# Attention scores of a hybrid layer: the low half of the keys in a whole 128-row tile

## The chip, the cores and the metric

The kernel runs on one core of one Trainium2 chip. The metric is the device time of one execution in microseconds (us). The engines are TensorE (PE; its weight loads stand apart as PEld), VectorE (DVE), ScalarE (ACT), GpSimd (POOL) and SyncE (SP), which issues the DMAs. Each works off its own queue in order and waits on the others by semaphores.

## The reference, cut to what matters

A sequence of 512 tokens with 1024 features goes through six sublayers with modulated norms (feed-forward, pooling, latent attention) and then through two hybrid layers. A hybrid layer has two attentions on one projection: stick-breaking attention (8 heads of 64) and native sparse attention (NSA: 8 query heads of 64 in 2 groups, each group with one head of keys and values). NSA has a compressed, a selected and a window branch. With 512 tokens there are 8 blocks of 64, and the 8 best are selected, which is all of them; the window has 512 tokens. So both branches are causal attention over all keys, each with its own keys:

```python
q = rope(rms_norm(split_heads(n_q, NSA_HEADS), q_norm_g), pos)
k_slc = rope(rms_norm(split_heads(n_ks, NSA_KV_HEADS), k_norm_g[1]), pos)
k_win = rope(rms_norm(split_heads(n_kw, NSA_KV_HEADS), k_norm_g[2]), pos)
...
ss = jnp.einsum('bgrqd,bgqkd->bgrqk', qb, ks) * scale
ps = masked_softmax(ss, (tok <= tq[:, None])[:, :, None])
o_s = jnp.einsum('bgrqk,bgqkd->bgrqd', ps.astype(vs.dtype), vs)
...
sw = jnp.einsum('bgrqd,bgkd->bgrqk', qb, kw) * scale
pw = masked_softmax(sw, mw)
o_w = jnp.einsum('bgrqk,bgkd->bgrqd', pw.astype(vw.dtype), vw)
```

## The kernel before, in words

Everything is float32 in value. A product is made of operands split in two, a high part h (rounded to the format in which TensorE multiplies) and a low part l, the rest. The program writes out the order of all work by hand: the instructions of each engine stand in its queue in the order in which the Python code issues them. A layer is a list of items (`Item`), and `drive` calls them one after the other and splits and loads weights a little ahead. The DMAs of weights stand on SP's queue.

**Selected and window branches.** There are 32 units a layer: 4 query heads j of a group, times 2 groups g, times 2 branches b (selected, window), times 2 halves gr of the queries. A unit has two query tiles of 128: gr 0 those that see 128 and 256 keys, gr 1 those that see 384 and 512. `attend` pipelines the units by steps in the order of the string NSO, "HES1LNPMO0T": S scores on TensorE (`NS`, for the unit one ahead), M row maximum on DVE (`NM`), E exponential on ACT (`NE`), N scaling on DVE and POOL (`NN`), T transposes on TensorE, H and L their evacuation and split on ACT and DVE, P product with the values on TensorE (three units behind), O fold of the result. The steps "1" and "0" are gaps in which other work stands, mostly quarters of projections for a gate (tile `gx`, L256 to L258). The scores of a gr 0 unit go to a single bank, tile `s`; those of gr 1 to the only pair of banks, tile `ps`.

**Where the scores' operands lie.** Queries and keys have 64 features, half of TensorE's 128 rows. The tile of a group's queries (qA, qB) holds on the 64 rows of the group (`rows(g)`) the high part and on the other 64 rows the low part. The tile of high keys, `kth` (`st["kh"]`), holds the same high part on both halves. So one product over 128 rows gives h·h + l·h. The third part, high queries with low keys, is a second product over the group's 64 rows alone; its keys are in `ktl` (`st["kl"]`), where the two groups lie in the two halves of the rows. `scores` (L1201) takes these terms: for each of the two query tiles it issues one product per term (L1208) and then adds the causal mask by a product with the identity (L1210 for gr 1, L1213 for gr 0), which has 128 rows. The queries are the operand that is loaded into the array (LDWEIGHTS), the keys the one that streams. In the stick-breaking attention the same function gets three terms that all have 64 rows (`S_`, L1380).

**Preparation.** `prep` (L1482) opens the pools of the branch when stick-breaking's are closed: `nsa` (P) for what lives on, `nsap` (PP) for what only the preparation needs, which closes at the first score unit; its room is then taken by `nsa2` with pA and pB, the split weights of the compressed branch. `prep` also loads `y`, the bias of the compression (L1500, later its hidden layer), and has `kr`, the compressed keys. Then it starts the norms and rotations of the keys and the first queries (`norm_rope`), whose powers are made on POOL (`rpow`, L277 and L278) and whose results DVE takes (L1134). `keys` (L1600) turns the keys, and writes `kth` on ACT and `ktl` on DVE (L1611).

Of the kernel before, what the change touches and what calls it, by code (L numbers as in the profile page):

```python
# [9 lines left out]
F32 = mybir.dt.float32  # L10
# [27 lines left out]
def band_constants():  # L38
    """Row tile j of the pooling matrices of the groups side by side, columns from BAND0[j]."""
    out = np.zeros((4, 128, BANDO[4]), np.float32)  # L40
    s = np.arange(S)
    for g, w in enumerate(WINDOWS):
        lo, hi = np.clip(s - w // 2, 0, S), np.clip(s + w // 2, 0, S)
        m = ((s[:, None] >= lo[None, :]) & (s[:, None] < hi[None, :])) / (hi - lo)[None, :]
        m = (m - np.eye(S)).astype(np.float32)
        for j in range(4):
            out[g, :, BANDO[j]:BANDO[j + 1]] = m[128 * j:128 * j + 128, BAND0[j]:BAND0[j] + BANDN[j]]
    return out


def constants():
    """Arrays that depend on the shapes alone."""
# [31 lines left out]
class Chunk:  # L84
    """One load of weights into a slot or two; parts: (destination view of the slots, source)."""
# [5 lines left out]
class Half:  # L91
    """A split operand of at most 1024 columns, from a part of a chunk; chunk None: only the room."""
# [13 lines left out]
class Kern:  # L106
# [22 lines left out]
    def cols(self, w, c0):  # L129
        """256 columns of w [1024, n]: halves of 128 columns, [128, 8, 128]."""  # L130
# [5 lines left out]
    def solo(shape, *parts, late=99, eng=None):  # L136
        """A half with a load of its own; parts: (columns of the slot, shape, source)."""
# [4 lines left out]
    def cols_k(self, w, c0):  # L142
        """256 columns of w [1024, n]: halves of four row tiles, [128, 4, 256]."""
        src = lambda m: w[512 * m:512 * m + 512, c0:c0 + 256].rearrange("(k p) n -> p k n", p=128)
        return [self.solo((4, 256), (slice(0, D), (4, 256), src(m))) for m in range(2)]

    def cols_q(self, w, c0):
        """128 columns of w [1024, n] from c0 and from c0 + 256: halves of four row tiles, [128, 4, 256]."""
# [8 lines left out]
    def rows_of(self, w, j):  # L157
        """Row tiles 2j and 2j + 1 of w [n, 1024]: halves of [128, 1024]."""
        return [self.solo((D,), (slice(0, D), (D,), w[j * 256 + m * 128:j * 256 + m * 128 + 128])) for m in range(2)]

    def place(self):
        """Where the next load goes: the next slot, or pair of slots, of a ring."""
# [73 lines left out]
    def warm(self, out, n):  # L236
        """Products of no use that keep the tensor engine's clock up through a wait; out [128, 512] is written anew afterwards."""
# [9 lines left out]
    def splits(self, *parts):  # L247
        """Splits whose sources may share a tile."""
# [11 lines left out]
    def mm2(self, out, v, xh, xl, start, stop):  # L260
        """out[0:64] + out[64:128] is the product; v [K, 128] holds h and l of 64 columns."""
# [4 lines left out]
    def fold(self, po, r, y=None):  # L266
        """po[0:64] + po[64:128] on the rows r of y or of a new tile."""
# [6 lines left out]
    def rpow(self, s, mul, add):  # L274
        """s <- (s * mul + add) ** -0.5, in place"""
# [12 lines left out]
    def take(self, tag):  # L288
        """Before a room is taken again, the chain that reads it is brought to its end."""
# [8 lines left out]
    def banks(self, kind=None):  # L298
        """PSUM: four pairs of banks; mla: two pairs and four single banks; hyb: a pair and six."""
# [7 lines left out]
    def scrt(self):  # L307
        """One of three rooms, of four in the second block."""
# [10 lines left out]
    def sigmoid_steps(self, dst, x, also=None):  # L319
        """dst <- exp(min(x, 0) - ln(1 + exp(-|x|)))."""  # L320
# [13 lines left out]
    def ada(self, i, j, which, g, m, form="row", pool=None, tiles=1, tag="adaw", ahead=0):  # L334
        """Steps towards modulation vector j of layer i: as rows, or as columns [128, 8] for rows later;
        itself (g None) or 1 + itself times the gains g."""
# [39 lines left out]
    def to_row(self, acc, which, g, m, gb=None):  # L376
        """The sum over partitions of acc [128, 1024] on every partition."""
# [25 lines left out]
    def spread(self, which, g, m):  # L403
        """Rows from columns."""
# [21 lines left out]
    def border(self, m, nxt):  # L426
        """The steps of a token tile into the next sublayer: scale of the norm, modulation, turn, split."""
# [42 lines left out]
    def finale(self, product, P1, Z, X, nxt, m2, kinds):  # L470
        """The last products of a sublayer token tile by token tile, with the border behind them.
        product(t, part) in two parts; P1, Z and X bring y into the residual."""
# [36 lines left out]
    def updater(self, m, kind):  # L509
        """x += weight * c * normed(y), or x += y / 4."""  # L510
# [21 lines left out]
    def out_items(self, w, part, last, before=None, after=None, late=99):  # L532
        """part(k) -> split [128, 512] of feature tile k; last(product)."""
# [129 lines left out]
    def pool(self, cur, last):  # L663
# [17 lines left out]
        def band(g, z, js, first, last_):  # L681
            """Tokens 256 z and on of the group's pooled input from the token tiles js."""
# [33 lines left out]
        def low(h, l, src, eng):  # L716
            """Only the first and the last token's eight divide by other than powers of two."""
# [18 lines left out]
        def scale(m):  # L736
            """The map and its bias times the channels' scale."""
# [34 lines left out]
    @staticmethod  # L772
    def parts(*parts):
        """A step's other work from (lane, function, weights, steps for which they stay)."""
# [6 lines left out]
    def attend(self, n, steps, order, slices):  # L781
        """Items of a pipeline over n units: steps[letter] = (function, offset), in the order given; digits:
        slices[step] = (lists of other work for the gaps, weights)."""
# [254 lines left out]
    def trig(self, ang, cos, sin, n, r):  # L1038
        """cos and sin of ang (float32), by a reduction with an exact split of 2 pi."""
# [23 lines left out]
    def trig_tables(self, C):  # L1063
        """Steps towards the cosines and sines of the second block."""
# [29 lines left out]
    def rope_rows(self, C, l):  # L1094
        """Rotary tables with the norms' gains inside: q, k of selection, k of window, compressed k."""
# [23 lines left out]
    def norm_rope(self, src, dst, tabs, c):  # L1119
        """Rows of src [128, t, h, 64] normed over 64 (c 1: and times 1 / 8), turned, into dst (same shape)."""  # L1120
# [22 lines left out]
    def chain(self, g, *tiles):  # L1143
        """Opens a chain of operations that reads the banks."""
# [7 lines left out]
    def follow(self, g):  # L1152
        """The next step of a chain."""
# [9 lines left out]
    def advance(self, n=1):  # L1163
        """The next step of every open chain of operations."""
# [9 lines left out]
    def chunk2(self, w, c0, c1, n=128):  # L1174
        """n columns of w [1024, m] from c0 and n from c1: two halves [128, 8, n]."""
# [3 lines left out]
    def token_proj(self, h, ws, ts, ps, o=0, heads=False):  # L1179
        """Token tiles ts x 256 columns into ps[:, t + o]; ws: halves of four row tiles; heads: columns (g, j, d) as (j, g, d)."""  # L1180
# [7 lines left out]
    def feat_proj(self, out, h, w, ks=range(8)):  # L1188
        """128 columns, features on partitions, [128, 512 tokens]."""
# [7 lines left out]
    def spans(self, g):  # L1197
        """The two query tiles of group g in a packed [128, 1024]."""
        return [slice(self.off(g, i), self.off(g, i) + 128 * (2 * g + i + 1)) for i in range(2)]

    def scores(self, terms, g, mask):  # L1201
        """Masked scores of the query tiles 2g and 2g + 1, packed side by side: sums of q^T k over terms (q, k)."""
# [13 lines left out]
    def turn_steps(self, un, U, P):  # L1216
        """Steps over units un[u] = {p: packed}: transposes, evacuation, product with the values."""
# [26 lines left out]
    def causal_pv(self, po, d, v, g, first, last):  # L1244
        """po [128, 256 queries of group g] += v^T p^T; v(k) [128 keys, h | l]."""
# [6 lines left out]
    def hybrid(self, cur, l, last):  # L1252
        """Items of a layer of the second block."""
# [5 lines left out]
        # -- stick-breaking attention  # L1259
# [30 lines left out]
        def FP(pr, z, ks, bank=None):  # L1290
            """Queries (z = 0) or keys of a pair of heads, row tiles ks; pr 4: inputs of the compression."""
# [24 lines left out]
        def GA(b, ks, bank=None):  # L1316
            """Columns of the first gate ahead of their turn."""
# [8 lines left out]
        def GZ(b, ks):  # L1326
            """Stick-breaking's gate for the heads 2b and 2b + 1, on their output."""
# [10 lines left out]
        def silu_chain(b, z):  # L1338
            """oa[:, b] *= 2 z sigmoid(z)"""
# [97 lines left out]
        def two(z, tags):  # L1437
            """A product with 256 columns, token tiles in two banks."""
# [13 lines left out]
        # -- native sparse attention: preparation  # L1452
# [13 lines left out]
        def q_chain(jp, ps, ts):  # L1466
            """Queries 2 jp and 2 jp + 1 of both groups, from ps [128, t, 256] (j, g, d)."""
# [14 lines left out]
        def prep(*ws):  # L1482
# [6 lines left out]
            st["kh"], st["kl"] = P.tile([128, 2, 2, 512], F32R, name="kth"), P.tile([128, 2, 512], F32R, name="ktl")  # L1489
# [6 lines left out]
            st["kr"] = P.tile([64, 64], F32, name="kr")  # L1496
            y = P.tile([128, 256], F32, name="y")
# [40 lines left out]
        def window(z):  # L1538
            """Keys and values of the window, gates of the branches, two token tiles."""
# [60 lines left out]
        def keys():  # L1600
# [8 lines left out]
            for b in range(2):  # L1609
                for g in range(2):  # L1610
                    nc.vector.tensor_tensor(st["kl"][rows(g), b], pt[b][rows(g)], st["kh"][rows(g), b, g].bitcast(F32), op=OP.subtract)  # L1611
# [94 lines left out]
        # -- native sparse attention: selected and window branches  # L1706
# [4 lines left out]
        def NS(u):  # L1711
# [5 lines left out]
            q, r = st["qB" if j > 1 else "qA"][g][:, j % 2], rows(g)  # L1717
            nu[u] = {"s": self.scores([(q, st["kh"][:, b, g]), (q[r], st["kl"][r, b])], gr, self.causal)}
# [56 lines left out]
        # -- gates, up-projections, output  # L1775
# [89 lines left out]
    def group(names, jobs):  # L1865
        """The jobs of the names one after the other, with their weights."""
# [8 lines left out]
    def open_x(self):  # L1875
        """Room of the residual."""
        self.x = self.xs.enter_context(self.tc.tile_pool(name="x", bufs=1, side="right")).tile([128, NT, D], F32, name="x")

    def park_x(self):
        """The residual leaves the core's memory while a layer of the second block needs the room."""  # L1880
# [212 lines left out]
```

## Time and profile before

| what | value |
|---|---|
| runs, us | 3033.26, 3033.55, 3036.77 (median 3033.55) |
| profiled execution, span | 3036.1 us; no other time of it is given |
| PE busy | 2888.1 us (95%) |
| PEld busy | 2403.2 us (79%) |
| DVE busy | 1612.7 us (53%) |
| ACT busy | 1164.8 us (38%) |
| POOL busy | 396.9 us (13%) |
| chain that ended last | PE 85%, DVE 8%, ACT 3%, POOL 2% |
| mean granted clock of TensorE | 0.960 |

The busy time of an engine is the sum over its instructions, the share is that of the span. Matmuls are pipelined and the profile models their ends, so a matmul's row overlaps the next one's; what a product costs in a row of products is the distance from its start to the next start. The granted clock is 1.00 at 2.4 GHz and 0.50 at 1.2 GHz. The chain that ended last is followed back from the last instruction, at each step to what released it. The runs lie within 0.12% of each other.

### The profile page before, as it was taken

How to read it: one execution, taken by the hardware profiler on the slowest of the kernel's cores; microseconds unless marked ns; L12 is line 12 of the kernel's file. 1: busy time of each engine (PE TensorE's matmuls, PEld its weight loads, DVE VectorE, ACT ScalarE, POOL GpSimd, SP SyncE). 2: the span in 40 equal slices, each digit the busy share in tenths (PEclk: the TensorE clock that was granted, in tenths of full speed). 3: DMA queues.
4: the chain of work that ended last, by engine and by line, in shares of the span. 5: the costliest groups of instructions: out<-in, count | busy, mean ns of one | idle time of the engine just before them, and what ended most of it. 6: DMA issues, size and time to landing. Idle time of an engine off the chain costs nothing.

```text
span 3036.1 us, 35669 instructions
## 1 busy us (share of the span) xinstructions
PE 2888.1 (95%) x14135; PEld 2403.2 (79%) x14135; DVE 1612.7 (53%) x2147; ACT 1164.8 (38%) x1946; POOL 396.9 (13%) x446
## 2 busy tenths in 40 slices
PE   7999988999999999899899999998999999889999
PEld 6888877888888888778788888787777887867787
DVE  6554355443364543579642234675665438756543
ACT  4223233222231222378422233563544338444431
POOL 1000031000010000267200000111230010112200
PEclk9999989999999999899999999998799999978999
DMA  7665313543246643110243332233102431320022
GB/s 260 217 196 166 110 59 113 179 156 115 88 130 206 215 160 94 33 41 15 84 153 98 103 111 71 75 94 85 29 15 84 146 93 57 88 64 28 28 94 100
DMA packets 232661, 322.60 MB, mean 106 GB/s; under 512 B 10823, under 2 KB 194331, under 8 KB 232494
## 3 DMA queue, kind: packets, MB, share of 16 engines
q1 hardware_dynamic: 230910, 314.55, 32.3%
q10 hardware_dynamic: 1584, 5.77, 0.5%
q8 instruction: 112, 1.84, 0.3%
q14 instruction: 55, 0.45, 0.0%
HBM read 313.99 MB, written 6.29 MB: 105 GB/s over the span
## 4 chain that ended last, share of the span: by engine, by line
PE 85%; DVE 8%; ACT 3%; POOL 2%; issue 2%; DMA 0%; POOLq 0%; SPq 0%; DVEq 0%; ACTq 0%
PE ps L256 21%; PE ps L257 21%; PE ps L258 21%; PE ps L1208 2%; PE gx L256 2%; PE gx L258 2%; PE gx L257 2%; PE pt L1227 2%; PE po L264 1%; PE s L1208 1%; PE po L263 1%; PE ps L1210 1%; DVE mx L970 1%; DVE wl L1006 1%; PE pt L1652 1%
## 5 line engine op out<-in xcount | busy, mean ns | idle before, releaser
L245 DVE TENSOR_TENSOR wl<-wraw,wh 128x1024 fp32r<-128x1024 f32 (+3 forms) x414 | 496.2, 1214 | 560.1 <-ACT wh L244 559.9
L256 PE MATMUL ps<-hh,wh 128*128 128x512 f32 (+1 forms) x1696 | 659.7, 389 | 8.2 <-DVE ob L271 2.8
L257 PE MATMUL ps<-hl,wh 128*128 128x512 f32 (+1 forms) x1696 | 657.4, 388 | 3.4 <-DVE hl L467 3.3
L258 PE MATMUL ps<-hh,wl 128*128 128x512 f32 (+1 forms) x1696 | 656.4, 387 | 0.6 <-DVE wl L245 0.5
L244 ACT ACTIVATE wh<-wraw 128x1024 fp32r<-128x1024 f32 (+4 forms) x430 | 435.2, 1041 | 572.8 <-PE ps L258 302.3
L256 PEld LDWEIGHTS ps<-hh,wh 128*128 128x128 f32 x1696 | 324.0, 191 | 74.2 <-DVE ob L271 4.2
L257 PEld LDWEIGHTS ps<-hl,wh 128*128 128x128 f32 x1696 | 323.8, 191 | 68.0 <-DVE hl L467 4.3
L258 PEld LDWEIGHTS ps<-hh,wl 128*128 128x128 f32 x1696 | 323.5, 191 | 65.4 <-DVE wl L245 1.2
L257 PE MATMUL ps<-wl,xh 128*128 128x512 f32 x800 | 315.1, 394 | 0.0
L256 PE MATMUL ps<-wh,xh 128*128 128x512 f32 x800 | 314.4, 393 | 0.0
L258 PE MATMUL ps<-wh,xl 128*128 128x512 f32 x800 | 311.2, 389 | 0.0
L361 DVE SCALAR_TENSOR_TENSOR acc<-adaw,sc,acc 128x1024 f32<-128x1024 f32 x144 | 188.6, 1310 | 120.0 <-DMA adaw<-in_ada_w_dram 118.8
L633 ACT ACTIVATE hid<-ps 128x1024 f32<-128x1024 f32 x44 | 45.2, 1027 | 478.9 <-PE ps L258 478.9
L277 POOL TENSOR_SCALAR s<-s 128x1 f32<-128x1 f32 x64 | 23.6, 368 | 1242.6 <-ACT junk L418 1241.6
L256 PEld LDWEIGHTS ps<-wh,xh 128*128 128x128 f32 x800 | 150.1, 188 | 34.9
L258 PEld LDWEIGHTS ps<-wh,xl 128*128 128x128 f32 x800 | 150.1, 188 | 33.9
L257 PEld LDWEIGHTS ps<-wl,xh 128*128 128x128 f32 x800 | 150.3, 188 | 30.6
L256 PE MATMUL gx<-hh,wh 128*128 128x512 f32 x304 | 128.3, 422 | 13.6 <-DVE oa L1342 7.0
L636 DVE TENSOR_TENSOR hid<-ps,hid 128x1024 f32<-128x1024 f32 x44 | 53.8, 1222 | 161.9 <-PE ps L258 161.8
L258 PE MATMUL gx<-hh,wl 128*128 128x512 f32 x304 | 125.1, 412 | 6.4 <-DVE wl L245 6.4
L257 PE MATMUL gx<-hl,wh 128*128 128x512 f32 x304 | 125.1, 412 | 0.0
L1739 POOL TENSOR_SCALAR scr<-scr,mx 128x256 f32<-128x256 f32 x64 | 86.7, 1355 | 253.6 <-DVE mx L1737 210.0
(483 smaller groups left out, 4855.8 us busy)
## 6 DMA issues: line engine op xcount, KB each, us to landing
wraw<-in_ffn_w_in_dram SPq DMA_DIRECT2D x88, 1024.0 KB, 5.2
adaw<-in_ada_w_dram SPq DMA_DIRECT2D x144, 512.0 KB, 6.1
wraw<-in_ffn_w_out_dram SPq DMA_DIRECT2D x88, 512.0 KB, 3.9
wraw<-in_w_in_dram SPq DMA_DIRECT2D x52, 512.0 KB, 4.6
wraw<-in_w_in_dram SPq DMA_DIRECT2D x14, 1024.0 KB, 5.2
wraw<-in_cmp_w_dram SPq DMA_DIRECT2D x16, 512.0 KB, 6.2
wraw<-in_w_out_dram SPq DMA_DIRECT2D x16, 512.0 KB, 3.8
adaw<-in_norm_g_dram ACTq DMA_DIRECT2D x11, 512.0 KB, 3.9
```

What stands on the lines that cost most here:

```text
L244: self.nc.scalar.activation(h, src, AF.Copy)
L245: (eng or self.nc.vector).tensor_tensor(l, src, h.bitcast(F32), op=OP.subtract)
L256: mm(out, w[0], x[0], start=start, stop=False)
L257: mm(out, w[0], x[1], start=False, stop=False)
L258: mm(out, w[1], x[0], start=False, stop=stop)
L263: mm(out, v, xh, start=start, stop=False)
L361: nc.vector.scalar_tensor_tensor(acc, raws[q][:, k], self.sc[:, f:f + 1], acc, op0=OP.mult, op1=OP.add)
L633: nc.scalar.activation(st["hid", it], ps, AF.Silu)
L636: nc.vector.tensor_tensor(h, ps, h, op=OP.mult)
L1208: mm(sc[:, f], q[:, c], k[:, 0:n], start=m == 0 and (g == 1 or i == 0), stop=False)
L1227: nc.tensor.transpose(t[:, k], d["p"][:, f.start + k * 128:f.start + k * 128 + 128], self.ident)
L1739: (nc.gpsimd if i == self.NNE else nc.vector).tensor_scalar(d["p"][:, f], d["p"][:, f], d["m"][:, 2 + i:3 + i], None, op0=OP.mult)
```

## The change

The low keys get a tile like that of the high keys: [128, 2, 2, 512], for each branch and group all 128 rows, the group's 64 with the low part and the other 64 zero. `prep` writes the zeros, one memset on POOL for each group; DVE's four subtractions write the group's rows of the new place. In `NS` the second product takes all 128 rows of the queries and of the low keys. The zero rows meet the low queries and add nothing, so the sum is as before. The tile grows by 4 KB a partition. `kr` (256 bytes) and `y` (1 KB) move from the pool that lives on to the one that closes at the first score unit. Nothing else is changed but comments and texts of functions, by which line numbers behind L1489 are two higher.

```diff
-            st["kh"], st["kl"] = P.tile([128, 2, 2, 512], F32R, name="kth"), P.tile([128, 2, 512], F32R, name="ktl")
+            st["kh"], st["kl"] = (P.tile([128, 2, 2, 512], F32R, name=n) for n in ("kth", "ktl"))
+            for g in range(2):
+                nc.gpsimd.memset(st["kl"][rows(1 - g), :, g].bitcast(F32), 0.0)
...
-            st["kr"] = P.tile([64, 64], F32, name="kr")
-            y = P.tile([128, 256], F32, name="y")
+            st["kr"] = PP.tile([64, 64], F32, name="kr")
+            y = PP.tile([128, 256], F32, name="y")
...
-                    nc.vector.tensor_tensor(st["kl"][rows(g), b], pt[b][rows(g)], st["kh"][rows(g), b, g].bitcast(F32), op=OP.subtract)
+                    nc.vector.tensor_tensor(st["kl"][rows(g), b, g], pt[b][rows(g)], st["kh"][rows(g), b, g].bitcast(F32), op=OP.subtract)
...
-            q, r = st["qB" if j > 1 else "qA"][g][:, j % 2], rows(g)
-            nu[u] = {"s": self.scores([(q, st["kh"][:, b, g]), (q[r], st["kl"][r, b])], gr, self.causal)}
+            q = st["qB" if j > 1 else "qA"][g][:, j % 2]
+            nu[u] = {"s": self.scores([(q, st["kh"][:, b, g]), (q, st["kl"][:, b, g])], gr, self.causal)}
```

On POOL, at the start of the preparation in the first hybrid layer, these rows stood (`wl` is the low half of a weight split, the tiles `r` hold the sums of squares that `rpow` takes):

```order
L1456 MEMSET scr 128x32 x2
L245 TENSOR_TENSOR wl<-wraw,wh 128x1024
L277 TENSOR_SCALAR r_14180<-r_14180 128x8
L278 TENSOR_TENSOR r_14180<-r_14180,mhalf 128x8
L277 TENSOR_SCALAR r_14182<-r_14182 128x8
L278 TENSOR_TENSOR r_14182<-r_14182,mhalf 128x8
```

With the change these rows stand there:

```order
L1456 MEMSET scr 128x32 x2
L245 TENSOR_TENSOR wl<-wraw,wh 128x1024
L1491 MEMSET ktl 64x2x512 x2
L277 TENSOR_SCALAR r_14182<-r_14182 128x8
L278 TENSOR_TENSOR r_14182<-r_14182,mhalf 128x8
L277 TENSOR_SCALAR r_14184<-r_14184 128x8
L278 TENSOR_TENSOR r_14184<-r_14184,mhalf 128x8
```

The two memsets stand behind the weight split and ahead of the first `rpow`; the second layer has the same. On TensorE the rows and their order stay, and so do the waits but for two in each layer. At the first product that reads pA (compressed branch, behind the value products of the first layer's fourth unit) it was, with the waits in brackets:

```order
L264 MATMUL po<-wl,nv_14129 128x256
L263 MATMUL po<-wh,nv_14129 128x128
L264 MATMUL po<-wl,nv_14129 128x128
L263 MATMUL po<-pAh,vc 128x512
L264 MATMUL po<-pAl,vc 128x512
```

And with the change:

```order
L264 MATMUL po<-wl,nv_14131 128x256
L263 MATMUL po<-wh,nv_14131 128x128
L264 MATMUL po<-wl,nv_14131 128x128
L263 MATMUL po<-pAh,vc 128x512 [waits DMAHW3_49,DMAHW2_49]
L264 MATMUL po<-pAl,vc 128x512
```

The waits for two DMA queues have moved here from the first product that reads `y0h`, behind the branches, which keeps its wait for a third queue and for ACT.

## Rows read from the trace of the kernel before

**Rows 1.** Windows: length, busy PE, PEld, DVE, ACT, POOL, then clock, DMA share, GB/s.

```profile
2132.09:2165.20 33.11, 31.86 (x110) 24.80 (x110) 24.81 (x56) 16.70 (x41) 7.54 (x6) 0.50 0.12 32
...
2189.44:2281.60 92.16, 92.16 (x491) 70.80 (x489) 56.92 (x156) 48.29 (x144) 27.99 (x21) 1.00 0.08 24
...
2766.33:2858.60 92.27, 92.27 (x491) 70.89 (x490) 56.70 (x156) 48.07 (x144) 28.00 (x21) 1.00 0.08 24
```

**Rows 2.** Timeline of PE, two units: start, us, tiles, rows*columns of the array, shape.

```profile
2198.94 0.30 PE L1208 MATMUL s<-kth,qAl 128*128 128x128 f32 x1
2199.17 0.33 PE L1208 MATMUL s<-ktl,qAl 64*128 64x128 f32 x1
2199.43 0.38 PE L1208 MATMUL s<-kth,qAl 128*128 128x256 f32 x1
2199.74 0.38 PE L1208 MATMUL s<-ktl,qAl 64*128 64x256 f32 x1
2200.05 0.39 PE L1213 MATMUL s<-causal,ones 128*128 128x256 f32 x1
2200.27 0.39 PE L256 MATMUL gx<-hh,wh 128*128 128x512 f32 x1
2200.50 0.40 PE L257 MATMUL gx<-hl,wh 128*128 128x512 f32 x1
...
2201.66 0.28 PE L263 MATMUL po<-wh,nv 128*128 128x256 f32 x1
2201.78 0.28 PE L264 MATMUL po<-wl,nv 128*128 128x256 f32 x1
...
2202.06 0.52 PE L1227 MATMUL pt<-ident,scr 128*128 128x128 f32 x3
2202.34 0.42 PE L1208 MATMUL ps<-kth,qAl 128*128 128x384 f32 x1
2202.68 0.44 PE L1208 MATMUL ps<-ktl,qAl 64*128 64x384 f32 x1
2203.05 0.33 PE L1210 MATMUL ps<-causal,ones 128*128 128x128 f32 x1
2203.22 0.45 PE L1208 MATMUL ps<-kth,qAl 128*128 128x512 f32 x1
2203.60 0.50 PE L1208 MATMUL ps<-ktl,qAl 64*128 64x512 f32 x1
2204.03 0.33 PE L1210 MATMUL ps<-causal,ones 128*128 128x128 f32 x1
2204.19 0.44 PE L256 MATMUL gx<-hh,wh 128*128 128x512 f32 x1
```

**Rows 3.** Timeline of PE in the stick-breaking attention, whose score products have 64 rows.

```profile
2008.50 0.33 PE L1208 MATMUL ps<-kl,qh 64*128 64x384 f32 x1
2008.67 0.33 PE L1208 MATMUL ps<-kh,ql 64*128 64x384 f32 x1
2008.93 0.33 PE L1210 MATMUL ps<-strict,ones 128*128 128x128 f32 x1
```

**Rows 4.** Timeline of PE, third and fourth unit of the first layer.

```profile
2145.79 0.45 PE L1208 MATMUL s<-kth,qAh 128*128 128x128 f32 x1
...
2147.97 0.84 PE L1227 MATMUL pt<-ident,scr 128*128 128x128 f32 x3
2150.07 0.69 PE L1208 MATMUL ps<-kth,qAh 128*128 128x384 f32 x1 [1.25 <-ACT scr L1730]
...
2153.23 0.65 PE L1674 MATMUL pt<-ident,scr 128*128 128x128 f32 x2
```

**Rows 5.** Groups of POOL by line and form: a memset of 1024 columns.

```profile
L339 POOL MEMSET acc<- 128x1024 f32 x18 | 17.2, 957 | 477.4 <-DVE wl L245 272.2 <-PE ps L368 205.1
```

**Rows 6.** Timeline of DVE at the preparation: the wait for POOL's `rpow`.

```profile
2046.98 0.69 DVE L1134 TENSOR_TENSOR scr<-ps,r 128x512 f32<-128x512 f32 x1 [1.57 <-POOL r L278]
```

**Rows 7.** Waits of PE from 2012 to 2135 us: total, times, longest.

```profile
PE gx L258 <- DVE wl L245: 3.3, 1, 3.3
```

## The prediction

> **What bounds the kernel now.** I read the windows by stage first, for the two stretches in which the changed products run, the selected and window branches of the two layers of the second block. In the dense part of it TensorE is busy for all of 92.16 us in the first layer and all of 92.27 in the second, at the full granted clock (1.00, 2.4 GHz), while DVE has 56.92 us of work, ACT 48.29 and POOL 27.99; the first 33.11 us have the half clock (0.50, 1.2 GHz) with TensorE busy for 31.86 [rows 1]. Busy time of matmuls is modelled, so I went on to their starts. The timeline of TensorE shows one unit with two query tiles of 128 and 256 keys, then one with 384 and 512 [rows 2]. No row in either carries a wait for another engine, yet the starts are far apart: the product of 384 columns with `kth` holds its place for 2202.68 - 2202.34 = 0.34 us and the one with `ktl` for 0.37. So what ends last in this stretch is TensorE's own sequence, and in it something that is no wait for data.
>
> What that is I took from the other attention of the same layer, whose score products all have 64 rows [rows 3]. There 384 columns that follow a product of the same height take 2008.67 - 2008.50 = 0.17 us, which is what 384 columns are at 2.4 GHz; the last one, before the 128-row mask, takes 0.26. The column counts are the same, the heights differ: a product costs its columns when its neighbours have its height, and 0.1 to 0.2 us more when they don't. In [rows 2] every step of a unit goes from 128 rows to 64 or back, except the step out of a mask. Taken for itself, a change of height is thus an extra pause on TensorE in these rows. The Trainium skill's page "TensorEngine Tiling (Array Packing)", section Key Properties, says the same in principle: a change of the tiling mode, not of the tile, drains the array; it gives no price, and none is needed here.
>
> **The change, part by part.**
>
> The products. Their number, order and columns stay, only the 64-row one becomes 128 rows high. A unit on two tiles of 128 and 256 keys takes 2200.27 - 2198.94 = 1.33 us to the start of what follows. With one height I price its five products by neighbours of one height in the same rows: 128 columns 0.10 (three transposes in 2202.34 - 2202.06 = 0.28), 256 columns 0.12 (2201.78 - 2201.66), so 2 x 0.10 + 3 x 0.12 = 0.56, which saves 0.77. A unit on 384 and 512 keys takes 2204.19 - 2202.34 = 1.85. With one height: 384 columns 0.17 twice [rows 3], 512 columns 0.23 twice (2200.50 - 2200.27), the mask of 128 columns 0.10 twice, together 1.00, which saves 0.85. A pair of units saves 1.62 us. Bounds of this price: 0.06 for a mask product whose weights came early would save 0.08 more a pair; nothing at all, if height is not the cause (a rival).
>
> How many of these lie on the path. Each layer has 32 units. The last 22 (11 pairs, the dense window begins with the first of them) run at the full clock [rows 1]: 11 x 1.62 = 17.8 us. They are followed by a drain that waits for the last fold, so the last pair's 1.6 may be lost there; I take 17.0 (range 16.2 to 17.8). That the other engines keep up I get from the same windows: 92.16 - 17.8 = 74.4 us is still well above DVE's 56.92.
>
> The first ten units run partly at the half clock. There a unit of the first kind takes 2147.97 - 2145.79 = 2.18 us and one of the second 2153.23 - 2150.07 = 3.16 [rows 4]. Twice the full-clock prices are 1.12 and 2.00, so they save 1.06 and 1.16. The row at 2150.07 shows a wait of 1.25 us for ACT's exponential of the unit two before. What the third unit (at 2145.79) saves, that wait takes back. The first two save 2.2, the fourth to sixth 3.4. The seventh to tenth I price at the full clock, 2 x 1.62 = 3.2. Sum 8.8; since the chain from ACT through POOL to the transposes is tight here, I take 8 (range 4.4 to 8.8).
>
> The two memsets. They are two rows more in POOL's queue, behind the weight split and ahead of all the `rpow` steps of the first keys and queries. They write 1024 values on each of 64 partitions; the nearest row is the memset of 128 x 1024, 0.957 us [rows 5]. Two are 1.9 us a layer. This is not covered: DVE's L1134 already waits 1.57 us for POOL's `rpow` [rows 6], behind it on DVE stand the norms, the rotations and the weight splits, and TensorE waits 3.3 us for one of these splits [rows 7]. All of that moves back by 1.9. The lower bound is nothing (if a later wait of TensorE took it up), the upper 4, twice the row, if the longer standstill costs TensorE its clock for a while. I take 2.0, a little over the row.
>
> What costs nothing. DVE's four subtractions into `ktl` keep shape and count, and stand on DVE's queue far behind operations that already need `rpow` results from behind the memsets, so the memsets are no wait for them. `kr` and `y` change pool: the room of `pA` now covers the place of `y`, and the first product that reads `pA` waits for two DMA queues where the first product of `y0h` did. These are the loads of `y`, whose values DVE's L1532 adds long before `pA` can exist (the compressed keys come out of them), so the wait is over when it is met. Were it not, TensorE would stand at that product with all units behind it.
>
> Sum for a layer: 17.0 + 8 - 2.0 = 23.0 us; two layers 46. Against the profiled execution, 3036.1 us of span (no time around it is given), that is 2990.1. This execution lies 2.55 us over the median of the runs, 3033.55, within their spread, so I predict 3033.55 - 46 = **2988 us**.
>
> **Rivals.**
>
> The clock turns earlier (chance 0.12). In the half-clock stretch of 33.11 us TensorE is busy for 31.86 by its records [rows 1], but much of this is pauses [rows 4]. With fewer pauses the full clock may come sooner. If a third of it (11 us) went to the full clock, 5.5 us a layer more are saved: 2977. Against it: the transposes in [rows 4] and the wait ahead of them stay.
>
> Half of it is given back (0.13). The chain T, H, E, S of a unit pair (transposes, ACT's evacuation, ACT's exponential, the next score product into the single pair of banks) gets shorter room by 0.77 us. Where ACT's exponential comes later than TensorE now wants the bank, the wait of 1.25 us in [rows 4] appears in every pair. For it: that wait exists already. Against: with 48.29 us of ACT work in 92.16 there is room. Half of the 50 us of products less the 4 of the memsets is 21: 3012.
>
> Height is not the cause (0.06). The pause could belong to two products that share one set of queries, or to accumulation into one bank. Then only the memsets count: 3033.5 + 3.8 = 3037, no change. Against: the 64-row products in [rows 3] accumulate the same way into one bank, without a pause.
>
> Slower: the 64-row products run beside their neighbours (0.05). Two products on different rows of the array could overlap, and a full-height one would then need a place of its own: 0.10 + 0.12 + 0.17 + 0.23 = 0.62 us a pair, 19.8 for 32 pairs, with the memsets 3057. It decides if a start behind a 64-row product comes sooner than the columns take; [rows 2] has 0.26 to 0.43 behind each, never less than the columns. The Trainium skill's page "TensorE: Matmul & The Clock Gate", section "Why this matters for your kernels", speaks for this one: it wants products of few rows sliced onto distinct row groups, where they run concurrently. By that rule padding is a loss; the trace has no pair of such neighbours here, since each 64-row product stands between two of 128.
>
> **How the numbers follow.** The forecast has 0.64; its own range comes from the bounds: 17.8 + 8.8 - 1.9 twice is 49 (2984), 16.2 + 4.4 - 4 twice is 33 (3000). The range 2974 to 3013 takes in the earlier clock and the half given back and leaves out the two last rivals, 0.11. About 0.2% (6 us) is what a measurement of this kernel can tell from no change. Faster: 0.64 + 0.12 + 0.13 = 0.89; within: 0.06; slower: 0.05.
>
> **What would show it.** In the profile after, the product with `ktl` has 128 rows, its 384 columns hold TensorE for 0.17 us and its 512 for 0.23, and a unit takes 0.56 and 1.00. The dense part of a layer is near 75 us instead of 92. POOL has two memsets of about 0.95 us ahead of the first `rpow`, and TensorE's wait behind L245 there is about 2 us longer. If the pauses stay with equal heights, the price fails. If they go and the dense part stays over 83 us, another engine has become the bound; a new wait for ACT's exponential or POOL's scaling would name it. If the half-clock stretch ends later or sooner than after 33 us less the savings in it, the clock has moved the result.

## The result and the profile after

| | before | changed |
|---|---|---|
| median of the runs, us | 3033.41 (4 runs, 3031.73 to 3036.77) | 2987.16 (4 runs, 2980.65 to 2992.45) |
| profiled execution, span, us | 3036.1 | 2986.2 |
| PE busy, us | 2888.1 | 2826.3 (95%) |
| POOL busy, us | 396.9 | 400.5 (13%) |
| mean granted clock | 0.960 | 0.964 |

The ratio is 0.9847, with a 95% interval from 0.9833 to 0.9862: 46.25 us less, where 46 was forecast. The predicted time, 2988, lies 0.8 us from the median. The terms of that sum fit less well than the sum does, so a fit as close as this is luck; the stages show it.

The windows of the changed kernel, with the columns of [rows 1]: the half-clock stretch from the first unit, the rest of the first ten units, and the dense parts of the first and second layer. The first line is from the kernel before: the rest of its first ten units, behind the half-clock stretch of [rows 1].

```profile
2165.20:2189.44 24.24, 24.24 (x120) 19.35 (x119) 15.01 (x39) 8.91 (x27) 5.30 (x4) 0.79 0.00 1
...
2134.19:2157.50 23.31, 20.44 (x86) 18.97 (x87) 20.77 (x43) 14.64 (x34) 4.92 (x4) 0.50 0.17 46
2157.50:2180.39 22.89, 21.74 (x142) 19.40 (x142) 17.29 (x49) 11.19 (x36) 6.93 (x5) 0.92 0.00 1
2180.39:2256.60 76.21, 76.21 (x492) 67.68 (x489) 56.18 (x159) 48.30 (x142) 28.42 (x22) 1.00 0.10 29
2733.36:2809.60 76.24, 76.24 (x492) 67.68 (x490) 56.20 (x159) 48.07 (x141) 28.42 (x22) 1.00 0.10 29
```

The dense parts were 92.16 and 92.27 long in [rows 1] and are 76.2 now, 16.0 us less in each. TensorE still fills them, DVE, ACT and POOL have nearly the same busy time as before, and none of them has become the bound. The half-clock stretch was 33.11 and is 23.31. A second, short one stands in the rest of the first ten units: 10.2 us before, 3.4 now (the clock of 0.79 and of 0.92 in these lines). It begins, before as after, in a row of products of only 32 columns (the compressed scores), without a wait ahead.

TensorE's timeline of the changed kernel, a unit with 384 and 512 keys, then one with 128 and 256, as in [rows 2]; start, us, tiles, rows*columns of the array.

```profile
2190.82 0.52 PE L1227 MATMUL pt<-ident,scr 128*128 128x128 f32 x3
2191.09 0.42 PE L1208 MATMUL ps<-kth,qAl 128*128 128x384 f32 x1
2191.35 0.34 PE L1208 MATMUL ps<-ktl,qAl 128*128 128x384 f32 x1
2191.53 0.22 PE L1210 MATMUL ps<-causal,ones 128*128 128x128 f32 x1
2191.59 0.45 PE L1208 MATMUL ps<-kth,qAl 128*128 128x512 f32 x1
2191.87 0.40 PE L1208 MATMUL ps<-ktl,qAl 128*128 128x512 f32 x1
2192.11 0.22 PE L1210 MATMUL ps<-causal,ones 128*128 128x128 f32 x1
2192.17 0.45 PE L256 MATMUL gx<-hh,wh 128*128 128x512 f32 x1
...
2195.18 0.31 PE L1208 MATMUL s<-kth,qAl 128*128 128x128 f32 x1
2195.33 0.28 PE L1208 MATMUL s<-ktl,qAl 128*128 128x128 f32 x1
2195.44 0.33 PE L1208 MATMUL s<-kth,qAl 128*128 128x256 f32 x1
2195.61 0.28 PE L1208 MATMUL s<-ktl,qAl 128*128 128x256 f32 x1
2195.72 0.29 PE L1213 MATMUL s<-causal,ones 128*128 128x256 f32 x1
2195.85 0.40 PE L256 MATMUL gx<-hh,wh 128*128 128x512 f32 x1
```

Read the distances of the starts. The `ktl` products now take 0.18 (384 columns), 0.24 (512), 0.11 (128) and 0.11 (256), near the 0.17, 0.23, 0.10 and 0.12 at which they were priced. The larger unit takes 2192.17 - 2191.09 = 1.08 (priced at 1.00, before 1.85), the smaller 2195.85 - 2195.18 = 0.67 (priced at 0.56, before 1.33). The 0.08 and 0.11 by which the units are longer than priced sit mostly in products that follow a narrow one (128 columns): `kth` with 384 columns behind the transposes 0.26 instead of 0.17, with 128 columns 0.15 instead of 0.10, with 256 columns behind one of 128 columns 0.17 instead of 0.12. The `kth` product of 512 columns behind a mask takes 0.28 instead of 0.23, but the mask takes 0.06 instead of 0.10.

POOL's timeline of the changed kernel at the preparation, and TensorE's waits from 2012 to 2137 (total, times, longest). Behind them stand two rows of the kernel before, from the window of [rows 7].

```profile
2041.30 2.65 POOL L245 TENSOR_TENSOR wl<-wraw,wh 128x1024 fp32r<-128x1024 f32 x1 [36.13 <-ACT wh L244]
2044.01 1.95 POOL L1491 MEMSET ktl<- 64x1024 f32 x2
2046.05 0.20 POOL L277 TENSOR_SCALAR r<-r 128x8 f32<-128x8 f32 x1
```

```profile
PE gx L256 <- DVE scr L1134: 4.6, 1, 4.6
...
PE gx L256 <- DVE oa L1342: 4.0, 1, 4.0
...
PE gx L258 <- DVE wl L245: 3.1, 1, 3.1
```

```profile
PE gx L256 <- DVE oa L1342: 3.6, 1, 3.6
...
PE gx L256 <- DVE scr L1134: 2.6, 1, 2.6
```

The two memsets take 1.95 us on 64 partitions, like 1.9 for two of the memsets on 128 in [rows 5]. The wait that grew is not the one I named: behind L245's split TensorE waits 3.1 instead of 3.3 [rows 7]; for L1134, the operation that takes `rpow`'s result [rows 6], it waits 4.6, which was 2.6 before.

### The profile page after: what moved, and what is told of

It reads as the page before. It is cut to its first block, busy times and chain, and to the rows that moved or that the text cites. A ratio compares the mean times of both kernels' runs of the same rounds, so it can differ in the third digit from the quotient of the medians.

```text
span 2986.2 us, 35675 instructions
## 1 busy us (share of the span) xinstructions
PE 2826.3 (95%) x14135; PEld 2383.9 (80%) x14135; DVE 1609.1 (54%) x2147; ACT 1166.3 (39%) x1946; POOL 400.5 (13%) x450
## 4 chain that ended last, share of the span: by engine, by line
PE 83%; DVE 8%; ACT 3%; POOL 2%; issue 2%; DMA 0%; POOLq 0%; SPq 0%; DVEq 0%; ACTq 0%
PE ps L256 22%; PE ps L257 22%; PE ps L258 21%; PE gx L256 2%; PE gx L258 2%; PE gx L257 2%; PE ps L1208 2%; PE pt L1227 2%; PE po L264 1%; PE po L263 1%; DVE mx L970 1%; DVE wl L1006 1%; PE s L1208 1%; PE pt L1654 1%; PE ps L368 1%
## 5 line engine op out<-in xcount | busy, mean ns | idle before, releaser
L245 DVE TENSOR_TENSOR wl<-wraw,wh 128x1024 fp32r<-128x1024 f32 (+3 forms) x414 | 496.6, 1215 | 557.6 <-ACT wh L244 557.2
L277 POOL TENSOR_SCALAR s<-s 128x1 f32<-128x1 f32 x64 | 23.4, 366 | 1242.6 <-ACT junk L418 1241.6
L256 PE MATMUL ps<-wh,hh 128*128 128x256 f32 (+3 forms) x352 | 112.0, 318 | 5.3 <-DVE scr L826 3.7
```

The source lines that it names most:

```text
L245: (eng or self.nc.vector).tensor_tensor(l, src, h.bitcast(F32), op=OP.subtract)
L256: mm(out, w[0], x[0], start=start, stop=False)
```

## Experiments

Each profiled execution was cut at the same places of a layer: POOL's weight splits ahead of the memsets (the start of the first of three), the first unit ("preparation" lies between), the eleventh unit (first ten units, "early"), the start behind the last mask ("dense"), and the next product of the stage behind. Times in us, first layer / second layer; the last two columns are the parts of "early" and of "preparation" with half the granted clock.

| kernel | preparation | early | dense | half clock in early | half clock in preparation |
|---|---|---|---|---|---|
| before | 93.53 / 92.94 | 57.35 / 57.31 | 92.22 / 92.27 | 43.4 / 43.3 | 21.5 / 21.6 |
| changed | 96.59 / 95.58 | 46.20 / 46.22 | 76.20 / 76.22 | 26.8 / 26.8 | 27.8 / 27.8 |
| e1_late_memsets | 93.23 / 92.77 | 46.20 / 45.35 | 76.23 / 76.23 | 26.7 / 22.7 | 24.5 / 18.3 |
| e2_tile_only | 96.51 / 94.13 | 52.00 / 57.19 | 92.22 / 92.22 | 30.3 / 43.0 | 27.7 / 21.8 |
| e3_by_height | 93.35 / 93.01 | 57.86 / 48.52 | 84.82 / 84.82 | 50.6 / 26.2 | 24.5 / 21.6 |
| e4_one_height_reordered | 95.97 / 95.56 | 46.19 / 46.20 | 76.09 / 76.06 | 26.7 / 26.8 | 28.0 / 27.8 |
| e5_wide_alone | 96.64 / 94.18 | 47.82 / 48.31 | 83.71 / 83.76 | 23.4 / 22.6 | 27.8 / 21.8 |
| e6_changed_again | 96.48 / 95.56 | 46.20 / 46.20 | 76.23 / 76.28 | 26.8 / 26.8 | 27.9 / 24.4 |
| e7_late_again | 93.21 / 92.78 | 45.35 / 45.36 | 76.22 / 76.22 | 22.6 / 22.7 | 21.8 / 18.2 |
| e8_memsets_thrice | 99.95 / 99.37 | 46.20 / 46.41 | 76.23 / 76.25 | 26.7 / 22.9 | 31.3 / 24.9 |

Up to that weight split all kernels have the same program, and the time to it lies between 2030 and 2039 us in these executions. That scatter is as large as many of the differences asked about, so stages are compared here and whole times only by their ratios. The kernels e1 to e4 ran on one chip (the kernel before there: 3029.49, 15 runs), e5 to e8 on another (3034.43, 9 runs).

**Tile, memsets and pools, but products of 64 rows** (e2_tile_only). Against the changed kernel:

```diff
-            q = st["qB" if j > 1 else "qA"][g][:, j % 2]
-            nu[u] = {"s": self.scores([(q, st["kh"][:, b, g]), (q, st["kl"][:, b, g])], gr, self.causal)}
+            q, r = st["qB" if j > 1 else "qA"][g][:, j % 2], rows(g)
+            nu[u] = {"s": self.scores([(q, st["kh"][:, b, g]), (q[r], st["kl"][r, b, g])], gr, self.causal)}
```

> The changed kernel with its large tile, memsets and pools, but the second score product takes 64 rows again, as before the change. Theory (the height of the product is the cause): the pauses are back, a unit takes 1.34 and 1.85 us at the full clock, and with the memsets the time is 3037, 4 us over the kernel before. Rival (the gain comes from where the tile lies or from the pools): 2987 to 2995.

Measured: 3029.38 (10 runs), ratio 0.9997 (0.9985 to 1.0009). The dense parts are back at 92.22 and the units at 1.34 and 1.85, so the height alone makes the gain there. The preparation is 3.0 and 1.2 us longer, but the whole is no slower. The windows of this kernel, early half-clock stretch and dense part of the first layer, and early half-clock stretch of the second:

```profile
2135.75:2159.25 23.50, 22.24 (x77) 17.40 (x77) 18.80 (x39) 13.08 (x29) 4.42 (x4) 0.50 0.17 45
...
2187.75:2279.97 92.22, 92.22 (x491) 70.85 (x490) 56.98 (x156) 48.28 (x145) 27.99 (x21) 1.00 0.08 24
2706.68:2739.50 32.82, 31.56 (x108) 24.50 (x109) 24.81 (x55) 16.45 (x41) 7.53 (x6) 0.50 0.12 33
```

The products are the same in both layers, yet the full clock comes back after 23.5 us in the one and after 32.8 in the other. In this execution the early part of the first layer is 5.3 us shorter for it, which is more than the 4.2 us of the two longer preparations. The expectation of +4 us missed this.

**Half the changes of height** (e3_by_height). The kernel before, its products of a unit grouped: both with `kth`, both with `ktl`, then the masks. A unit has two changes of height instead of four.

```diff
+    def scores_by_height(self, terms, g, mask):
...
+        for m, (q, k) in enumerate(terms):
+            for i, f in enumerate(self.spans(g)):
+                c, n = tok(2 * g + i), f.stop - f.start
+                mm(sc[:, f], q[:, c], k[:, 0:n], start=m == 0 and (g == 1 or i == 0), stop=False)
...
-            nu[u] = {"s": self.scores([(q, st["kh"][:, b, g]), (q[r], st["kl"][r, b])], gr, self.causal)}
+            nu[u] = {"s": self.scores_by_height([(q, st["kh"][:, b, g]), (q[r], st["kl"][r, b])], gr, self.causal)}
```

> The kernel before (64 rows, no memsets) with the products of a unit in another order: both 128-row products, then both 64-row products, then the mask. Four changes of height in a unit become two, with the same products. Theory (each change of height costs about 0.18 us, 0.7 to 0.8 for the four of a unit): a unit saves half of that, 0.37 us; the dense part of a layer is 84 us instead of 92, and the time is near 3009 (3003 to 3015). Rival (the pause belongs to two products in a row with the same queries into the same place): it is gone altogether, units of 0.7 and 1.1 us, 2980 to 2985. Rival (a 64-row product is slow by itself): no change, 3033.

Measured: 3002.15 (4 runs), ratio 0.9909 (0.9888 to 0.9929). Its timeline of TensorE in the dense part, both kinds of unit:

```profile
2196.14 0.51 PE L1242 MATMUL pt<-ident,scr 128*128 128x128 f32 x3
2196.41 0.66 PE L1222 MATMUL ps<-kth,qAl 128*128 128x384 f32 x2
2196.99 0.67 PE L1222 MATMUL ps<-ktl,qAl 64*128 64x384 f32 x2
2197.59 0.44 PE L1225 MATMUL ps<-causal,ones 128*128 128x128 f32 x2
2197.86 0.44 PE L256 MATMUL gx<-hh,wh 128*128 128x512 f32 x1
...
2200.88 0.47 PE L1222 MATMUL s<-kth,qAl 128*128 128x128 f32 x2
2201.28 0.49 PE L1222 MATMUL s<-ktl,qAl 64*128 64x128 f32 x2
2201.70 0.38 PE L1228 MATMUL s<-causal,ones 128*128 128x256 f32 x1
2201.92 0.39 PE L256 MATMUL gx<-hh,wh 128*128 128x512 f32 x1
```

The units take 1.45 and 1.04 us, half-way between before (1.85, 1.33) and changed (1.08, 0.67), with the low products still 64 rows high. The dense part is 84.82, 7.4 us less than before and 8.6 more than with the change:

```profile
2184.48:2269.30 84.82, 84.82 (x491) 67.73 (x490) 56.32 (x155) 47.91 (x143) 27.99 (x21) 1.00 0.08 26
```

The whole came out some 7 us under the expected 3009, on a chip whose runs of before are 4 us lower too.

**The same order with one height** (e4_one_height_reordered). The changed kernel with the grouped order of e3, as the control for the order.

```diff
-            nu[u] = {"s": self.scores([(q, st["kh"][:, b, g]), (q, st["kl"][:, b, g])], gr, self.causal)}
+            nu[u] = {"s": self.scores_by_height([(q, st["kh"][:, b, g]), (q, st["kl"][:, b, g])], gr, self.causal)}
```

> The changed kernel with the order of products of the kernel that groups by height (both with the high keys, both with the low keys, then the mask). Control for that order. Theory (order matters by changes of height alone, and here there are none): units of 0.66 and 1.07 us as in the changed kernel, 2987 within the scatter of the runs. Rival (order matters by itself): 5 us or more away.

Measured: 2981.65 (4 runs), ratio 0.9839 (0.9826 to 0.9853); dense 76.09 and 76.06 against 76.20 and 76.22. The median lies 5.5 us under the changed kernel's 2987.16, but on the chip whose runs of before are 4 us lower; the ratios, 0.9839 and 0.9847, agree within their intervals. Without changes of height the order is worth 0.1 to 0.2 us a layer of dense part. What e3 gained, it gained by the changes that it saves.

**One kind of unit alone** (e5_wide_alone). The full height only for the units of 384 and 512 keys.

```diff
-            nu[u] = {"s": self.scores([(q, st["kh"][:, b, g]), (q, st["kl"][:, b, g])], gr, self.causal)}
+            r = slice(0, 128) if gr else rows(g)
+            nu[u] = {"s": self.scores([(q, st["kh"][:, b, g]), (q[r], st["kl"][r, b, g])], gr, self.causal)}
```

> The changed kernel, but only the units on 384 and 512 keys have the full-height product; those on 128 and 256 keys take 64 rows. Theory (pauses by unit): units of 1.34 and 1.07 us, the dense part of a layer is 92.2 less 11 x 0.78 = 83.6 us; with 5 us less in the first ten units and 2.8 more for the memsets each layer saves 11, the time is 22 us under the kernel before (ratio 0.9925, 0.991 to 0.995). Rival (one change of height in a unit in each kind is enough to spoil the sequence, or another engine takes up the room): dense part 88 us or more.

Measured: 3001.51 (4 runs), ratio 0.9889 (0.9875 to 0.9902). The dense part is 83.71, that is 8.5 us less than before or 0.77 for each of eleven units, and 7.5 more than with the whole change, 0.68 for each of the eleven others. The two kinds add up. The ratio is lower than the expected 0.991 to 0.995 because of the early part, 47.82 instead of 57.35 although only five of its ten units are changed; the half clock took 23.4 us of it instead of 43.4.

**The memsets elsewhere** (e1_late_memsets, and once more on the other chip as e7_late_again). They stand behind the one of `kcl`, where POOL has nothing to do.

```diff
-            for g in range(2):
-                nc.gpsimd.memset(st["kl"][rows(1 - g), :, g].bitcast(F32), 0.0)
...
             nc.gpsimd.memset(lo.bitcast(F32), 0.0)
             for g in range(2):
+                nc.gpsimd.memset(st["kl"][rows(1 - g), :, g].bitcast(F32), 0.0)
+            for g in range(2):
```

> The changed kernel, but POOL writes the zeros of the low keys' tile later, behind the memset of the compressed keys, where POOL has nothing to do for some 27 us. Theory (the memsets delay the chain of rpow, norms and weight splits): the first rpow starts right behind the weight split again, TensorE's wait for L1134 is 2.6 us as before the change and not 4.6, the first score unit starts 2.1 us earlier in each layer, and the time falls by 4 us, from 2987 to 2983. Rival (a later wait takes the delay up): the first unit starts at the same place and the time stays at 2987.

> The kernel with the memsets moved to where POOL is idle, once more, beside the changed kernel. From the weight split on POOL to the first score unit the changed kernel took 96.6 and 95.6 us in its two layers, this kernel 93.2 and 92.8. Theory (the memsets stand on the chain): 5 to 6 us less than the changed kernel, ratio 0.0018 lower. Rival (given back before the dense part, as the kernel with the tile alone suggests, which was no slower than the kernel before): less than 2 us.

Measured: 2979.3 (5 runs), ratio 0.983 (0.9815 to 0.9844); on the other chip 2978.99 (5 runs), ratio 0.9819 (0.9805 to 0.9832). POOL's timeline of e1_late_memsets, and the row of TensorE's waits that answers to the 4.6 above:

```profile
2106.20 0.14 POOL L1593 MEMSET kcl<- 128x64 f32 x1
2106.40 1.95 POOL L1595 MEMSET ktl<- 64x1024 f32 x2
2133.03 0.93 POOL L1741 TENSOR_SCALAR scr<-scr,mx 128x256 f32<-128x256 f32 x1 [24.68 <-DMA wraw<-in_w_in_dram]
```

```profile
PE gx L256 <- DVE scr L1134: 2.6, 1, 2.6
```

The memsets cost the same 1.95 us on POOL, with a gap of 24.68 behind them, and the wait is back at 2.6. The preparation is 93.23 and 92.77, shorter by 3.4 and 2.8 than in the changed kernel, where 2.1 were expected, and no longer than before the change. This is the fastest version.

**The changed kernel again** (e6_changed_again), beside e7 on the same chip.

> The changed kernel once more, beside the two kernels that differ from it in the memsets alone, since times of the same kernel differ from chip to chip. Its ratio to the kernel before is to be 0.984 to 0.985 again.

Measured: 2987.95 (4 runs), ratio 0.9842 (0.9829 to 0.9856). The late memsets lie 9 us under it, where 5 to 6 were expected; the stages hold 6.1 of preparation and 1.7 of early part (3.27 + 2.78, and 0.85 + 0.84), 7.7 in all.

**Six memsets instead of two** (e8_memsets_thrice), ahead of the first `rpow`.

```diff
-            for g in range(2):
+            for g in (0, 1, 0, 1, 0, 1):
                 nc.gpsimd.memset(st["kl"][rows(1 - g), :, g].bitcast(F32), 0.0)
```

> The changed kernel with each memset of zeros written three times, so six of them stand ahead of the first rpow and not two. Theory (they stand on the chain): TensorE's wait for L1134 grows by 4 x 0.97 = 3.9 us to 8.5, from the weight split to the first unit a layer takes 99.5 to 100.5 us, and the time is 8 us over the changed kernel (6 to 11, with the clock). Rival (taken up later): within 2 us of it.

Measured: 2993.34 (4 runs), ratio 0.9863 (0.985 to 0.9877), 5.4 us over e6_changed_again by the medians. POOL's timeline and TensorE's wait:

```profile
2044.95 5.96 POOL L1491 MEMSET ktl<- 64x1024 f32 x6
```

```profile
PE gx L256 <- DVE scr L1134: 8.6, 1, 8.6
```

Four more memsets are 4.0 us on POOL, the wait grows by 4.0 and the preparation by 3.5 and 3.8: nearly one for one, 7.3 us by stages. The 5.4 of the medians is less than the 6 to 11 expected; the part of the program ahead of the weight split scatters by more than that difference.

The change of pools was not tried by itself, nor were 64-row products as neighbours on different rows.

## Why the prediction came out right

**Height is the cause.** Four changes of height in a unit, two, or none: 92.2, 84.8 and 76.2 us in the dense part. Order without height gives 0.1 to 0.2 (e4), tile and pools without height nothing there (e2), half of the units half of it (e5). One change costs 16.0 / (11 x 8) = 0.18 us at the full clock. That settles the rival "height is not the cause" and, as the time fell, the one of 64-row products that run beside their neighbours; but whether two such neighbours on different rows would run together no run here shows. The Trainium skill's page "TensorEngine Tiling (Array Packing)", section Key Properties, states that changing the tiling mode, not just the tile, drains TensorE. The trace agrees that the change costs time, by these three lengths of one stage; that it is a drain, or that a change of tile alone is free, no run here shows.

**The dense part** was taken at 17.0 (range 16.2 to 17.8) and is 16.0, just outside. The price of a pair, 1.62, was too high: by the rows it is 1.33 + 1.85 = 3.18 before less 0.67 + 1.08 = 1.75 after, 1.43, and by the stage 16.0 / 11 = 1.46. I had priced each product by a neighbour of the same width and so missed what a product behind a narrow one takes. All eleven pairs count in full, so nothing was lost at the end of the last pair, and nothing was given back there: the windows show TensorE busy throughout. For the dense part the rival "half of it is given back" is out.

**The early part** was taken at 8 (range 4.4 to 8.8) and is 11.1, and here the step failed in kind, not only in size. The third unit's saving went where I said: the wait for ACT's exponential, 1.25 in [rows 4], is 2.23 now, 0.98 longer.

```profile
2150.02 0.69 PE L1208 MATMUL ps<-kth,qAh 128*128 128x384 f32 x1 [2.23 <-ACT scr L1732]
```

More waits came that I had not counted. These are TensorE's in the branches of the first layer; of these two rows the kernel before had only the 1.25:

```profile
PE ps L1208 <- ACT scr L1732: 2.6, 2, 2.2
PE pt L1227 <- DVE wl L1240: 1.3, 2, 0.7
```

So 1.3 us for DVE's splits of the transposes and 0.4 more for ACT's exponential are new, and with the 0.98 the waits take 2.7 us back. In this part the rival "half of it is given back" has some truth.

And the clock had been held fixed, but it moved. By the sign that I gave, the half-clock stretch of 33.11 should have lost the 2.2 + 3.4 priced in it and ended after 27.5; it ended after 23.31. I had also priced the tenth unit at the full clock, while it stands in the second half-clock stretch, before as after (3.15 us then, 1.96 now). Both stretches together had 43.4 us before and have 26.8 after. Two kernels in which the same products met either level show what that can be worth: e2 with 30.3 and 43.0 us of it took 52.00 and 57.19, e3 with 26.2 and 50.6 took 48.52 and 57.86, so 0.41 and 0.38 us for each us at the half clock. By 0.4, the 16.6 us less would be 6.6 us of the gain. That is an upper estimate, since part of the 16.6 went because the products in them became shorter. The distances of the starts in both traces, product by product in the first layer, part it better: score products that met the same clock in both kernels take 8.5 us less, other products at the same clock 0.7 more, the waits 2.7 more, and the products that met the half clock before and the full clock now take 6.0 less, 3.8 of it in other products and 2.2 in score products, which lost pauses too. So the clock is worth 3.8 to 6.0 us, and the pauses less the waits 5.1 to 7.3. The rival "the clock turns earlier" (5.5 us a layer) came true beside the forecast.

Why the clock comes back when it does stays open: in e2, with nothing changed in the products, it came back sooner in one layer and not in the other, and in e3 later in one and sooner in the other. The twelve early parts with the full height in all units had 22.6 to 26.8 us at the half clock, the six with 64 rows in all units 26.2 to 50.6. So less half clock goes with the height, but that the height moves the clock is argued, not shown.

**The memsets** were taken at 2.0 and cost 3.06 and 2.64. POOL's part was right, 1.95; they are not covered, as e1 and e8 show. The wait behind L245, which I gave as the sign, did not grow. The wait behind L1134 grew by 2.0, the price of the forecast. The rest goes in the main with the clock: the preparation had the half clock for 21.5 us before and for 27.8 with the change. By the starts, the first layer lags 2.0 us behind the kernel before at that wait, then 1.2 once its products have met the full clock sooner, then 3.0 once they have met the half clock again. In the second layers of e2 and e5, with 21.8 us of half clock and the same wait, the memsets cost 1.2. My upper bound of 4 had allowed for the clock, the 2.0 had not. Why the clock fell there is not shown.

**The sum.** Two layers: 32.1 of dense part, 22.2 of early part, 5.7 of memsets, so 48.6 by stages, where the prediction had 34, 16 and 4. The spans differ by 49.9 (0.96 of it ahead of the preparation, where nothing is changed), the medians by 46.25. The dense part and the memsets came out worse by 3.6 together, the early part better by 6.2. With the clock of the early part as before, the same terms would have made some 37 to 41, and 2988 would have been missed by 5 to 9 us, still inside the range. So the range and the main cause were right, and the 0.8 us by which 2988 was missed rests on errors that cancelled. The fixed time around the span, not given beforehand, is 1.8 us (2987.97 for a span of 2986.2).

## What to carry to other kernels

Look at the distance of matmul starts where TensorE is busy all the time: a product that holds its place longer than its columns need, with no wait in its row, is a cost of the sequence. If its neighbours use another number of rows, give it theirs by zero rows, or, where there is no room for that, group products by height; both can be priced from rows of the same trace. Put the zeros where the engine that writes them has a gap: the same two memsets lengthened the two preparations by 5.7 us ahead of a tight chain, and not at all some 70 us later.

## What had not been expected of the hardware

A product of 64 rows, by itself between products of 128, is dearer than one of 128 with half of its rows zero: 0.43 us for 512 columns [rows 2] became 0.24 at the same clock, and the 128-row product ahead of it went from 0.38 to 0.28. A memset on 64 partitions takes as long as one on 128 (0.95 and 0.957 us for 1024 values each). And the granted clock of a stretch is no property of its products: the same ten units had between 26.2 and 50.6 us at half of it in one execution (e3), which moved them by 9.3 us.
